# The first layer's output projection multiplies plain float32 operands once per product instead of rounded halves three times

## The chip, the cores and the metric

The kernel runs on one core of a Trainium2 chip, in one launch. The metric is device microseconds of that launch. The core's engines are TensorE (PE; its weight loads are shown apart as PEld), VectorE (DVE), ScalarE (ACT), GpSimd (POOL) and SyncE (SP), which here issues nearly all of the DMAs.

## What is computed

Two layers of a decoder trunk with three parallel attention branches. The sequence has 512 tokens, the model has 1024 channels, and everything is float32. The reference, cut to the lines that matter here:

```python
for layer in range(DEPTH):                       # DEPTH = 2
    h = rmsnorm(x, norm_g[layer])
    u = jnp.einsum('bsd,dc->bsc', h, w_in[layer])
    ... # three branches ya, yb, yc and their gates ga, gb, gc come out of u
    merged = (jax.nn.sigmoid(ga) * jnp.einsum('bsc,cd->bsd', ya, w_br_a[layer])
              + jax.nn.sigmoid(gb) * jnp.einsum('bsc,cd->bsd', yb, w_br_b[layer])
              + jax.nn.sigmoid(gc) * jnp.einsum('bsc,cd->bsd', yc, w_br_c[layer]))
    x = x + jnp.einsum('bsd,de->bse', merged, w_out[layer])
return rmsnorm(x, final_norm_g)
```

The change touches the product of `merged` with `w_out` for layer 0 alone: a matrix of 512 tokens by 1024 channels times one of 1024 by 1024.

## The kernel before, in words

Activations lie transposed, with 128 channels on the partitions and the 512 tokens along the free dimension. A matrix of 1024 channels is 8 tiles of 128x512.

**Three products for one.** Nearly every matmul works on numbers split in two: a high half, which is the value rounded to the type float32r, and a low half, which is what the rounding left, again as float32r. A product of two such numbers is three matmuls into the same accumulator, high by high, high by low and low by high (`mm3`, L125 to L128). An output tile of a projection is one accumulation over 8 channel tiles, 24 matmuls (`run_unit`).

**The weight stream.** All weights lie packed in one array, in blocks of 128x512 or so, in the order of their use. `dma_to` loads a block into a tile `raw`, of which there are 5 buffers (RAW). `split_to` makes the block's high half on ACT (a cast, L905) and its low half on DVE (a subtraction, L907), each into one of 6 buffers `wh` and `wl` (RING). This runs up to 6 blocks ahead of the matmuls. A `raw` buffer is free again when DVE has subtracted.

**The end of layer 0.** The last merge step for channel tile i (`m_item`, branch 2) leaves the finished sum `M[i]` in a float32 tile `mg`. ACT casts it to its high half (L605) and DVE subtracts for the low half (L606). These 16 half tiles lie in buffers named `qk` and `y`. Then comes the output projection, `o_item(e)` for e = 0 to 7. Each uses two weight blocks, named here oe-a (k = 0 to 3) and oe-b (k = 4 to 7). Its output is added to the residual, which was loaded as `xr` into a tile named `sz` (L626). The sum is stored to DRAM as `x1d` (L629), split for the next layer into `XH[e]` on ACT and `XL[e]` on DVE, and squared for the norm. Between these items stand the first steps of layer 1: `v_item(1, e-1)` is 12 matmuls with `XH[e-1]` and `XL[e-1]` and one more weight block (L229 to L231), named here v0 to v7. The order on PE is o0, o1, v0, o2, v1 and so on to o7, v6, v7. The norm's sums (L172) follow, then the step `va_item` with four blocks f0 to f3 (L256 to L258).

**What sets the order.** The kernel records its steps in a list and writes them out in that order, with the loads and splits of later blocks put between. A scheduler of the tile framework then orders each engine's queue and gives buffers out. Each engine works its queue strictly in order. SP issues the weight loads, the `xr` loads and the `x1d` stores from one queue.

**Plain float32 in the kernel before.** Three small products have both operands in plain float32: the norm's column sums (L172, 128x1, 16 matmuls in the program), the cumulative sum (L294, 128x16, 2 in the program) and its carries (L299, 128x12, 128x8 and 128x4, 6 in the program). L499, L323 and L213 are transposes.

The functions of the kernel before, where the diff touches them:

Of the kernel before, what the change touches and what calls it, by code (L numbers as in the profile page):

```python
# [13 lines left out]
P = 128  # L14
# [3 lines left out]
KT = 8  # L18
# [13 lines left out]
def _chunks():  # L32
    """Every weight block, in the order of the packed array: (key, floats per partition)."""
    out = []
    for l in range(L):
        for k in range(KT):
            out.append((("v", l, k), 512))
        for j in range(4):
            out.append((("f", l, j), 520))
        cols = []  # L40
        for n, w in (("qa", 2), ("ka", 2), ("za", 2), ("qb", 3), ("kb", 3), ("zb", 3),
                     ("qc", 3), ("kc", 1), ("zc", 3), ("ga", 8), ("gb", 8), ("gc", 8)):
            cols += [COL[n] + P * i for i in range(w)]
        for c in cols:
            for h in range(2):
                out.append((("u", l, c, h), 512))
        for br in range(3):
            for i in range(8):
                out.append((("p", l, br, i), P * NBR[br]))
        for e in range(8):  # L50
            for h in range(2):
                out.append((("o", l, e, h), 512))
    return out
# [11 lines left out]
def tile_trunk(ctx: ExitStack, tc: tile.TileContext, xT, wpk, gT, gfT, bfg, snk,  # L65
               mask_a, mask_b, mask_c, ident_d, upper_d, cos_d, sin_d, out):
    nc = tc.nc
# [13 lines left out]
    def mm_bank():  # L81
        return PS("mm", 3)
# [12 lines left out]

# [1 line left out]
    def const(src, shape, tag):  # L97
# [9 lines left out]

# [1 line left out]
    items = []  # L109
# [30 lines left out]

# [1 line left out]
    XH, XL = [None] * KT, [None] * KT  # L142
    st = {}
# [31 lines left out]
    def rms_post(tbs=range(4)):  # L175
        """1/sqrt(mean + eps) by token: a first guess from the bits, then Newton's steps."""
        c = slice(tbs[0], tbs[-1] + 1)
        v, t, vh = (T([P, 4], F32, n)[:, c] for n in ("rv", "rt", "rh"))
        seed = T([P, 4], I32, "r0")[:, c]
        st["r"] = T([P, 4], F32, "r")  # L180
        r = st["r"][:, c]
        nc.vector.tensor_scalar(v, st["ss"][:, c], 1.0 / D, EPS, op0=ALU.mult, op1=ALU.add)
        nc.vector.tensor_scalar(seed, v.bitcast(I32), -0.5, float(0x5F3759DF), op0=ALU.mult, op1=ALU.add)
        nc.vector.tensor_scalar(vh, v, -0.5, None, op0=ALU.mult)
        y = seed.bitcast(F32)
        for _ in range(3):
            nc.vector.tensor_tensor(t, y, y, op=ALU.mult)
            nc.vector.tensor_tensor(t, t, vh, op=ALU.mult)
            nc.vector.scalar_tensor_tensor(r, t, 1.5, y, op0=ALU.add, op1=ALU.mult)
            y = r  # L190

    def rms_root(tbs):
        """The same from the square root's table, with one of Newton's steps."""
        c = slice(tbs[0], tbs[-1] + 1)
        v, t, y = (T([P, 4], F32, n)[:, c] for n in ("rv", "rt", "rh"))
        st["r"] = T([P, 4], F32, "r")
        ss = st["ss"][:, c]
        nc.scalar.activation(y, ss, AF.Sqrt, scale=1.0 / D, bias=st["eps"])
        nc.vector.tensor_scalar(v, ss, -0.5 / D, -0.5 * EPS, op0=ALU.mult, op1=ALU.add)
        nc.vector.reciprocal(y, y)  # L200
        nc.vector.tensor_tensor(t, y, y, op=ALU.mult)
        nc.vector.tensor_tensor(t, t, v, op=ALU.mult)
        nc.vector.scalar_tensor_tensor(st["r"][:, c], t, 1.5, y, op0=ALU.add, op1=ALU.mult)
# [15 lines left out]

# [1 line left out]
    def v_item(l, k):  # L221
# [108 lines left out]

# [1 line left out]
    def qk_tile():  # L332
# [7 lines left out]
    def rope_1(ps):  # L340
        """The normalised values, their halves swapped, and the cosine's part."""
        x, sw, t = plain(ps), tmp(), tmp()
        for a, b in ((0, 32), (32, 0), (64, 96), (96, 64)):
            nc.sync.dma_start(sw[a:a + 32, :], x[b:b + 32, :])
        nc.gpsimd.tensor_tensor(t, x, st["cos"], op=ALU.mult)  # L345
        return t, sw
# [5 lines left out]
    def q_fill(t, h, aug):  # L352
        """Both heads' stacked q from t: high halves beside low halves."""
        for o in range(2):
            a, b = slice(HD * o, HD * o + HD), slice(HD - HD * o, 2 * HD - HD * o)
            q = st["QS", h + o] = qk_tile()
# [18 lines left out]

    # A projection is (chunks, pe, p1, p2, p3): the work of the other engines in three parts.
    def qk_item(l, kind, n, h):
        """Projection unit n of a kind of columns, whose heads are h and h+1."""
        rope = kind[1] != "a"
        fill = q_fill if kind[0] == "q" else k_fill  # L380
        d = {}
# [17 lines left out]

# [1 line left out]
    def z_item(l, kind, n, pair):  # L401
# [15 lines left out]

# [1 line left out]
    NSB = (2, 2, 3, 4)  # L419
# [148 lines left out]

# [1 line left out]
    def m_item(l, br, i):  # L570
# [18 lines left out]
        def p2():  # L589
# [7 lines left out]
            if br == 1:  # L597
                nc.gpsimd.tensor_tensor(m, m, gr, op=ALU.add)  # L598
                return
            nc.vector.tensor_tensor(m, m, gr, op=ALU.add)  # L600
            pair = []
            for w in range(2):
# [6 lines left out]

# [1 line left out]
    def load_res(e):  # L611
# [3 lines left out]
    def o_item(e):  # L615
        d = {}

        def pe(HL):
            if e == 0:
                load_res(0)  # L620
                load_res(1)
            d["ps"] = run_unit(HL, [st["MH", i] for i in range(8)], [st["ML", i] for i in range(8)])

# [10 lines left out]

    # The last layer's output projection goes by halves of the tokens, so that one half's norm and
    # store run beside the other half's products.
    HT = S // 2
# [80 lines left out]

# [1 line left out]
    xs = [T([P, S], F32, "mg", 8) for _ in range(KT)]  # L720
# [6 lines left out]
    def layer(l):  # L727
        if l == 0:
            for k in range(KT):
                v_item(0, k)  # L730
        # the later layers' V steps stand among the output projection's of the layer before
        pe, post, ch = va_item(l)
# [72 lines left out]
        a3, b_prev, v_prev = [], [], None  # L805
        # Scores run a head ahead of their transposes: h is the head whose scores follow.
        for h in range(17):
# [64 lines left out]

# [1 line left out]
    seq = [c for it in items for c in it[0] or ()]  # L874
# [12 lines left out]
    def places(key):  # L887
        """Where a block's two halves go; the last projection's all stay, where others have left."""
        n = 2 * key[2] + key[3] if key[:2] == ("o", L - 1) else 0
# [9 lines left out]
    def split_to(n):  # L899
        while ptr["split"] < min(n, len(seq)):  # L900
            i = ptr["split"]
            w = off[seq[i]][1]
            h, lo = places(seq[i])
            r = raw.pop(i)
            (nc.vector.tensor_copy if i == 0 else nc.scalar.copy)(h[:, :w], r[:, :w])  # L905
# [135 lines left out]
```

## Time and profile before

| What | Value |
|---|---|
| Median of 2 timed runs | 893.16 us (892.62 and 893.71) |
| Span of the profiled execution, first to last instruction | 891.6 us |
| What lies between that span and the median | 1.6 us |
| TensorE busy | 880.3 us, 99% of the span |
| VectorE busy | 607.0 us, 68% |
| ScalarE busy | 463.5 us, 52% |
| GpSimd busy | 127.4 us, 14% |
| Granted TensorE clock, mean | 0.996 of full speed |
| Share of PE in the chain that ended last | 97% |

The profiled execution has no time of its own on record besides its span; the two timed runs lie 1.0 and 2.1 us above it. Matmuls are pipelined: a row's duration reaches from the start of one matmul to its modelled end and overlaps with the next one's. What a matmul costs in a stream is therefore read from start to start.

### The profile page before, as it was taken

The page shows a single profiled execution, that of the slowest core. Times are in us where ns is not written, and L with a number is a line of the kernel's source. Part 1 is how long each engine was busy: PE and PEld are TensorE (multiplying, and loading weights), DVE is VectorE, ACT ScalarE, POOL GpSimd, SP SyncE. Part 2 cuts the span into 40 slices and gives each one's busy share as a digit, 9 for nine tenths or more (in the row PEclk, how much of TensorE's full clock was granted, in tenths as well). Part 3 has the DMA queues.
Part 4 walks back from the last instruction along what each step waited for, and adds up shares of the span by engine and source line. Part 5 has one row for each costly group of instructions (what it writes and reads, how often), then busy time and mean ns, then how long its engine had stood idle before and what let it go on. Part 6 is the DMA issues. An engine that isn't in the chain of part 4 may idle for free.

```text
span 891.6 us, 12997 instructions
## 1 busy us (share of the span) xinstructions
PE 880.3 (99%) x4432; PEld 740.6 (83%) x4432; DVE 607.0 (68%) x1280; ACT 463.5 (52%) x964; POOL 127.4 (14%) x98
## 2 busy tenths in 40 slices
PE   9999999999999999999999999999999999999996
PEld 7988888888888888888889888888888888888895
DVE  7658899898775646554445879999886655555433
ACT  7477566665554434334335766666554544333542
POOL 5000131211001110001120012212100111100531
PEclk9999999999999999999999999999999999999998
DMA  6532323323232323335542233233322332233423
GB/s 217 175 106 72 107 72 89 99 80 95 74 98 80 91 86 108 89 104 166 146 138 84 83 86 87 77 101 101 83 83 77 87 89 82 82 98 92 129 79 113
DMA packets 53875, 89.26 MB, mean 100 GB/s; under 512 B 7344, under 2 KB 15920, under 8 KB 53808
## 3 DMA queue, kind: packets, MB, share of 16 engines
q1 hardware_dynamic: 53664, 88.42, 34.6%
q8 instruction: 35, 0.57, 0.3%
q14 instruction: 32, 0.26, 0.1%
q10 hardware_dynamic: 144, 0.01, 0.0%
HBM read 78.96 MB, written 4.19 MB: 93 GB/s over the span
## 4 chain that ended last, share of the span: by engine, by line
PE 97%; DVE 1%; DMA 0%; issue 0%; ACT 0%; POOL 0%; DVEq 0%; ACTq 0%; POOLq 0%
PE mm L127 26%; PE mm L126 26%; PE mm L128 26%; PE pv L545 4%; PE att L499 3%; PE att L435 2%; PE att L434 2%; PE att L229 2%; PE att L230 2%; PE att L231 2%; PE mm L256 1%; PE mm L257 1%; PE mm L258 1%; DMA g<-in_gT_dram 0%; PE pv L172 0%
## 5 line engine op out<-in xcount | busy, mean ns | idle before, releaser
L126 PE MATMUL mm<-xh,wh 128*128 128x512 f32 x736 | 293.1, 398 | 0.0
L905 ACT CAST wh<-raw 128x512 fp32r<-128x512 f32 (+3 forms) x277 | 163.4, 593 | 246.9 <-PE mm L127 191.6
L128 PE MATMUL mm<-xh,wl 128*128 128x512 f32 x736 | 290.5, 395 | 0.0
L127 PE MATMUL mm<-xl,wh 128*128 128x512 f32 x736 | 290.0, 394 | 0.0
L907 DVE TENSOR_TENSOR wl<-raw,wh 128x512 fp32r<-128x512 f32 (+3 forms) x272 | 182.4, 672 | 66.7 <-ACT wh L905 65.9
L128 PEld LDWEIGHTS mm<-xh,wl 128*128 128x128 f32 x736 | 138.2, 188 | 32.6
L127 PEld LDWEIGHTS mm<-xl,wh 128*128 128x128 f32 x736 | 138.4, 188 | 30.4
L126 PEld LDWEIGHTS mm<-xh,wh 128*128 128x128 f32 x736 | 138.4, 188 | 30.1
L470 ACT ACTIVATE P<-P,ng 128x256 f32<-128x256 f32 (+3 forms) x128 | 67.0, 525 | 38.0 <-DVE ng L468 38.0
L586 DVE TENSOR_TENSOR tmp<-mm,rbc 128x512 f32<-128x512 f32 x48 | 33.1, 690 | 55.9 <-PE mm L128 55.9
L345 POOL TENSOR_TENSOR tmp<-tmp,cos 128x512 f32<-128x512 f32 x20 | 31.3, 1566 | 258.1 <-DVE tmp L337 241.6
L127 PE MATMUL mm<-y,wh 128*128 128x512 f32 (+1 forms) x156 | 60.1, 385 | 0.3 <-DVE y L606 0.3
L126 PE MATMUL mm<-y,wh 128*128 128x512 f32 (+1 forms) x156 | 60.3, 386 | 0.0
L128 PE MATMUL mm<-y,wl 128*128 128x512 f32 (+1 forms) x156 | 60.0, 385 | 0.0
L598 POOL TENSOR_TENSOR mg<-mg,tmp 128x512 f32<-128x512 f32 x16 | 25.8, 1611 | 235.9 <-DVE tmp L596 235.9
L525 DVE TENSOR_TENSOR PL<-att,PH 128x512 fp32r<-128x512 f32 (+2 forms) x84 | 46.5, 598 | 0.1
L587 ACT ACTIVATE tmp<-tmp 128x512 f32<-128x512 f32 x48 | 30.4, 634 | 23.7 <-DVE tmp L586 23.6
L596 DVE SCALAR_TENSOR_TENSOR tmp<-tmp,mm 128x512 f32<-128x512 f32 x32 | 22.0, 687 | 28.8 <-PE mm L128 27.6
L524 ACT CAST PH<-att 128x512 fp32r<-128x512 f32 (+2 forms) x84 | 39.5, 526 | 2.4 <-PE att L499 1.2
L488 DVE TENSOR_SCALAR P<-P,den 128x256 f32<-128x256 f32 (+3 forms) x128 | 38.4, 364 | 1.1
L435 PE MATMUL att<-qk,qk 128*128 128x256 f32 (+2 forms) x128 | 37.1, 309 | 0.1
L499 PEld LDWEIGHTS att<-ident,P 128*128 128x128 f32 x284 | 32.9, 141 | 4.1
(197 smaller groups left out, 1376.6 us busy)
## 6 DMA issues: line engine op xcount, KB each, us to landing
raw<-in_wpk_dram SPq DMA_DIRECT2D x232, 256.0 KB, 2.7
raw<-in_wpk_dram SPq DMA_DIRECT2D x32, 192.0 KB, 2.4
tmp<-tmp SPq DMA_DIRECT2D x80, 64.0 KB, 2.0
raw<-in_wpk_dram SPq DMA_DIRECT2D x8, 260.0 KB, 2.7
mg<-in_xT_dram SPq DMA_DIRECT2D x8, 256.0 KB, 5.6
raw<-in_wpk_dram SPq DMA_DIRECT2D x16, 128.0 KB, 2.1
sz<-in_xT_dram SPq DMA_DIRECT2D x8, 256.0 KB, 3.0
x1d<-tmp SPq DMA_DIRECT2D x8, 256.0 KB, 3.3
```

What stands on the lines that cost most here:

```text
L126: nc.tensor.matmul(ps, wh, xh, start=first, stop=False)
L127: nc.tensor.matmul(ps, wh, xl, start=False, stop=False)
L128: nc.tensor.matmul(ps, wl, xh, start=False, stop=last)
L435: nc.tensor.matmul(ps, q2[:, qs], k2[:, a:a + n], start=False, stop=True)
L470: nc.scalar.activation(pb, pb, AF.Exp, bias=ng[:, i:i + 1], scale=-1.0, accum_out=den[:, i:i + 1])
L488: nc.vector.tensor_scalar(blks[i], blks[i], den[:, i:i + 1], None, op0=ALU.mult)
L499: nc.tensor.transpose(ps[:, c * P:(c + 1) * P], pt[:, src * P:(src + 1) * P], st["ident"])
L524: nc.scalar.copy(hh, bk[:, :n])
L525: nc.vector.tensor_tensor(st["PL"][:, o:o + n], bk[:, :n], rd(hh), op=ALU.subtract)
L545: nc.tensor.matmul(ps[:, q:q + n], v[j], src[:, o:o + n], start=w == 0 and m == 0, stop=w == 1 and m == 3)
L905: (nc.vector.tensor_copy if i == 0 else nc.scalar.copy)(h[:, :w], r[:, :w])
L907: eng.tensor_tensor(lo[:, :w], r[:, :w], rd(h[:, :w]), op=ALU.subtract)
```

## The change

For layer 0 alone, the sum `M[i]` is no longer split, and the blocks of the output projection are no longer split. The projection's matmul takes the `raw` block and the tile `M[k]`, both plain float32, in one matmul per product. `split_to` hands a `raw` tile of this projection on as it is. Layer 1 keeps the three products. The diff, cut to its core (the rest of it removes comments and blank lines):

```diff
@@ m_item, p2
             nc.vector.tensor_tensor(m, m, gr, op=ALU.add)
+            if l == 0:
+                return
             pair = []
@@ o_item, pe
-            d["ps"] = run_unit(HL, [st["MH", i] for i in range(8)], [st["ML", i] for i in range(8)])
+            ps = d["ps"] = mm_bank()
+            for k in range(KT):
+                w = HL[k // 4][0]
+                nc.tensor.matmul(ps, w[:, (k % 4) * P:(k % 4 + 1) * P], st["M", k], start=k == 0, stop=k == KT - 1)
@@ split_to
             w = off[seq[i]][1]
+            r = raw.pop(i)
+            if seq[i][:2] == ("o", 0):
+                hl[i] = (r, r)
+                ptr["split"] += 1
+                continue
             h, lo = places(seq[i])
-            r = raw.pop(i)
```

In PE's queue, this is where the last merge step ends and o0 begins. In the names, `mm` is the accumulator, `y` and `qk` are halves of activations, `wh` and `wl` halves of weights. Before:

```order
L128 MATMUL mm_3991<-y_3544,wl_3948 128x512
L126 MATMUL mm_4032<-qk_3590,wh_4001 128x512
L127 MATMUL mm_4032<-qk_3591,wh_4001 128x512
L128 MATMUL mm_4032<-qk_3590,wl_4002 128x512
L126 MATMUL mm_4032<-qk_3650,wh_4001 128x512
L127 MATMUL mm_4032<-qk_3651,wh_4001 128x512
L128 MATMUL mm_4032<-qk_3650,wl_4002 128x512
```

And with the change, from the same place to the last two products of o1 and the first matmuls of v0:

```order
L128 MATMUL mm_3963<-y_3544,wl_3924 128x512
L627 MATMUL mm_3988<-mg_1717,raw_3871 128x512
L627 MATMUL mm_3988<-mg_1822,raw_3871 128x512
...
L627 MATMUL mm_4018<-mg_2727,raw_3929 128x512
L627 MATMUL mm_4018<-mg_2819,raw_3929 128x512
L229 MATMUL att_4047<-wh_3997,xh_877_4010 128x512
L230 MATMUL att_4047<-wl_3998,xh_877_4010 128x512
```

Each run of three rows has become one row, 64 rows in place of 192, and the steps keep their order on PE.

In SP's queue, this is a stretch of the weight loads in the first items of the projection, with what each load waits for in brackets. Before:

```order
L883 DMA raw_4069<-in_wpk_dram 128x512 [waits DMAHW0_49,DVE_49]
L883 DMA raw_4071<-in_wpk_dram 128x512 [waits DMAHW1_49,DVE_49]
L883 DMA raw_4084<-in_wpk_dram 128x512 [waits DMAHW2_49,DVE_49]
L883 DMA raw_4119<-in_wpk_dram 128x512 [waits DMAHW3_49,DVE_49]
L613 DMA sz_4075<-in_xT_dram 128x512 [waits DVE_49]
L629 DMA x1d<-tmp_4073 128x512
```

With the change (raw_3973 and raw_3975 are o2-a and o2-b, raw_3982 is v1, raw_4001 and raw_4003 are o3-a and o3-b, raw_4016 is v2):

```order
L888 DMA raw_3973<-in_wpk_dram 128x512 [waits DMAHW1_49,DVE_49]
L888 DMA raw_3975<-in_wpk_dram 128x512 [waits DMAHW5_49,PE_49]
L888 DMA raw_3982<-in_wpk_dram 128x512 [waits DMAHW6_49,PE_49]
L615 DMA sz_4007<-in_xT_dram 128x512 [waits DVE_49]
L634 DMA x1d<-tmp_4005 128x512
L888 DMA raw_4001<-in_wpk_dram 128x512 [waits DMAHW7_49,PE_49]
L888 DMA raw_4003<-in_wpk_dram 128x512 [waits DMAHW4_49,DMAHW0_49,DVE_49]
L888 DMA raw_4016<-in_wpk_dram 128x512 [waits PE_49]
L615 DMA sz_4035<-in_xT_dram 128x512 [waits DMAHW2_49,DVE_49]
```

Before, every weight load waits for DVE's subtraction of the block that held the buffer. Now two of three wait for PE, since the block of the projection stays in its buffer until its four matmuls are done: o2-b waits for the last matmul of o0-a, v1 for the last of o0-b, o3-a for the last of o1-a, v2 for the last of o1-b. The `xr` loads and `x1d` stores stand behind them.

## Rows read from the trace of the kernel before

**Rows 1.** The page's head and its first part, busy time by engine.
```profile
span 891.6 us, 12997 instructions
PE 880.3 (99%) x4432; PEld 740.6 (83%) x4432; DVE 607.0 (68%) x1280; ACT 463.5 (52%) x964; POOL 127.4 (14%) x98
```
**Rows 2.** Waits of PE in the whole run, all there are.
```profile
PE pv L917 <- DVE qk L914: 1.5, 1, 1.5
PE pv L213 <- DVE r L203: 1.3, 1, 1.3
PE pv L172 <- ACT tmp L676: 0.8, 1, 0.8
PE att L229 <- ACT ys L161: 0.7, 1, 0.7
PE mm L127 <- DVE y L606: 0.3, 1, 0.3
```
**Rows 3.** Busy time by engine from o0's first matmul to the norm's sums.
```profile
398.87:465.66 66.79, 66.79 (x289) 54.06 (x288) 29.84 (x44) 25.48 (x41) 9.93 (x10) 1.00 0.52 151
```
**Rows 4.** Instruction groups in that stretch: busy, mean, then idle before and its releasers.
```profile
L126 PE MATMUL mm<-qk,wh 128*128 128x512 f32 x48 | 18.9, 394 | 0.0
...
L907 DVE TENSOR_TENSOR wl<-raw,wh 128x512 fp32r<-128x512 f32 (+1 forms) x24 | 16.5, 689 | 20.3 <-ACT wh L905 20.3
L905 ACT CAST wh<-raw 128x512 fp32r<-128x512 f32 (+1 forms) x24 | 14.9, 622 | 36.0 <-PE mm L127 29.3 <-ACT tmp L164 6.0 <-ACT ys L161 0.6
```
**Rows 5.** Timeline of all engines around o0's start: start, duration, what.
```profile
398.87 0.40 PE L126 MATMUL mm<-qk,wh 128*128 128x512 f32 x1
...
400.34 0.68 DVE L600 TENSOR_TENSOR mg<-mg,tmp 128x512 f32<-128x512 f32 x1
...
401.71 0.69 DVE L606 TENSOR_TENSOR y<-mg,y 128x512 fp32r<-128x512 f32 x1 [0.69 <-ACT y L605]
```
**Rows 6.** PE groups by shape, whole run: float32r products, then plain float32 ones.
```profile
L545 PE MATMUL pv<-PL,vb 128*128 128x256 f32 x72 | 12.4, 281 | 0.0
L545 PE MATMUL pv<-PL,vb 128*128 128x512 f32 x12 | 4.8, 396 | 0.0
...
L299 PE MATMUL pv<-lf,ones 128*128 128x12 f32 x4 | 0.7, 259 | 0.0
L299 PE MATMUL pv<-lf,ones 128*128 128x8 f32 x4 | 0.7, 256 | 0.0
L299 PE MATMUL pv<-lf,ones 128*128 128x4 f32 x4 | 0.7, 253 | 0.0
L294 PE MATMUL pv<-lf,upper 128*128 128x16 f32 x4 | 0.6, 220 | 0.0
```
**Rows 7.** One line, L172: duration in ns (min, median, max).
```profile
L172 PE MATMUL pv<-ones,ys x24: 164/250/251, 30.2 to 882.7; 128*128 128x1 f32 x24
```
**Rows 8.** Timeline of PE around the first cumulative sum.
```profile
48.53 0.39 PE L128 MATMUL mm<-xh,wl 128*128 128x512 f32 x1
48.76 0.29 PE L294 MATMUL pv<-lf,upper 128*128 128x16 f32 x2
48.90 0.81 PE L299 MATMUL pv<-lf,ones 128*128 128x12 f32 x6
49.57 0.48 PE L126 MATMUL mm<-xh,wh 128*128 128x512 f32 x1
49.88 0.39 PE L127 MATMUL mm<-xl,wh 128*128 128x512 f32 x1
```
**Rows 9.** Timeline of the weight loads at the same place.
```profile
48.53 0.42 PEld L294 LDWEIGHTS pv<-lf,upper 128*128 128x128 f32 x2
48.87 0.75 PEld L299 LDWEIGHTS pv<-lf,ones 128*128 128x128 f32 x6
```
**Rows 10.** Weight-load groups by shape, whole run: float32r, then plain float32.
```profile
L126 PEld LDWEIGHTS mm<-xh,wh 128*128 128x128 f32 x736 | 138.4, 188 | 30.1
...
L172 PEld LDWEIGHTS pv<-ones,ys 128*128 128x128 f32 x24 | 3.3, 191 | 0.2
```
**Rows 11.** DMA issues, 395 to 480 us: count, size, median us to landing.
```profile
raw<-in_wpk_dram SPq DMA_DIRECT2D x27, 256.0 KB, 2.7
```

## The prediction

> **What bounds the kernel now.** I read the page's busy times first. PE is busy 880.3 of 891.6 us [rows 1]. The waits of PE say where the rest is: five waits, 4.6 us in all [rows 2], and what is left lies before the first and behind the last matmul. So the kernel is bound by the number and length of its matmuls. The reader should see that none of the five waits is in the projection itself: the one for L606 is of a later place, since in the stretch of the projection PE is busy for 66.79 of 66.79 us [rows 3].
>
> That stretch is the one to price. Its window begins with o0's first matmul and ends with the norm's sums, and holds the 192 matmuls of o0 to o7 and the 96 of v0 to v7 (the row's 289th is one that reaches in from ahead) [rows 3]. 66.79 us over 288 is **231.9 ns from start to start**. The mean of 394 ns that the group rows give [rows 4] is start to modelled end and overlaps with the next matmul, so it is not what one costs.
>
> **What is removed on PE.** 192 matmuls of 231.9 ns are 44.5 us. They lie fully on the path.
>
> **What is added on PE.** 64 matmuls of plain float32, 128x512. The trace of before has none of that width, and the nearest rows are the three small float32 products. Two things can be seen in them.
>
> First, one of them in the program is two in the trace. The program has 2 of L294, 6 of L299 and 16 of L172; the trace has 4 of L294 and three groups of 4 of L299, 12 in all [rows 6], and of L172 24 of the 12 that read `ys` [rows 7]. Each of the two has a weight load of its own: 2 loads for the one L294, 6 for the three L299 [rows 9]. So 64 matmuls in the program will be **128 in the trace**.
>
> Second, each of the two takes longer per column. For float32r, 256 columns have a duration of 281 ns and 512 have 396 [rows 6], which is 115/256 = 0.449 ns per column. (512 of those are 230 ns, which agrees with the 231.9 from start to start, so the growth of the duration with the columns is the rate, plus some 2 ns.) For float32 L299 has 253 ns at 4 columns, 256 at 8 and 259 at 12 [rows 6], and L172 250 at 1 [rows 7]: 9/11 = 0.82 ns per column, 1.8 times as much. The rows are rounded to a nanosecond, so that the slope may be 0.73 to 0.91; L294 (220 at 16) mixes a first and a second matmul and doesn't fit a line. A slope of that size means that each of the two streams its columns **at about half the rate**.
>
> So one matmul of 512 columns in the trace takes between 512 x 0.82 + 2 = 422 ns and, at exactly half the rate of float32r, 2 x 231.9 = 464 ns. I take the middle, 443 ns, as neither end has a better claim. A product is then 0.886 us (0.844 to 0.928), and 64 are **56.7 us** (54.0 to 59.4). A step from at most 16 columns to 512 is a long one, and this is the term on which the forecast rests. The Trainium skill speaks against the change here: "FP8 and Floating Point Precision", section "TensorE Precision Notes", says that true float32 takes four passes through the array, one for each pair of halves. No row here shows passes as such; by it the sum is an estimate of 64 x 4 x 231.9 ns = 59.4 us.
>
> **Switching between the types.** Behind the last L299 the first float32r matmul starts at 49.57 and the next one at 49.88, 0.31 us instead of 0.23 [rows 8]: 0.08 us more. The other way, from L128 to L294, it is 48.53 to 48.76, the usual 0.23 [rows 8]. The new order has seven changes from float32 to float32r (from o1 to v0, then from each of o2 to o7 to its v step), so 7 x 0.08 = **0.6 us**.
>
> **What goes from ACT and DVE.** 16 casts and 16 subtractions of weight blocks at 622 and 689 ns [rows 4], and eight of each for the sums M. This is some 24 x 0.62 = 15 us of ACT and 24 x 0.69 = 17 us of DVE. I cost it at nothing: PE, which is the bound, waits for neither in that stretch [rows 3], where they are busy for 25.48 and 29.84 of 66.79 us. The earlier M sums gain nothing either. Before, M[7] is summed from 400.34 to 401.02 and its low half is there at 402.40 [rows 5]; o0 asks for them as its eighth product, 7 x 0.695 = 4.9 us after 398.87. With the change it asks for M[7] at 398.87 + 7 x 0.886 = 405.1, 4 us after it is there.
>
> **What is moved on the queue of SP.** A block of the projection now holds its `raw` buffer until its matmuls are done, so that two of three weight loads wait for PE, with the `xr` loads and `x1d` stores queued behind them. Is a block late? A load lands 2.7 us after its issue [rows 11], and a v block then needs 0.62 us of ACT and 0.69 us of DVE [rows 4], 4.0 us in all. With products of 0.886 us an o item lasts 7.1 us and a v step 12 x 0.232 = 2.8 us. Block v1 waits for the end of o0, and is used after o1, v0 and o2, 17 us later. The `xr` tile of item 3 stands behind block v2, which waits for the end of o1; it is used at the end of o3, behind v0, o2, v1 and o3, 20 us later. The tightest is the row v6, v7, f1, which share one buffer: v6 waits for the end of o5, v7 for DVE's subtraction of v6, f1 for that of v7, at some 4.4 us each with the issue. f1's cast stands on ACT ahead of the split of o6's output, so that split comes 12 to 13 us after the end of o5; v6 uses it v4, o6, v5 and o7 after that end, 19.8 us. That leaves 6 us. So this costs 0, with 0 and 6 us as its ends, since a slip of the supply could not exceed the slack by more than one load and its split.
>
> **The sum.** 56.7 + 0.6 - 44.5 = **+12.8 us**, from 10.1 (54.0 + 0.6 - 44.5) to 15.5 (59.4 + 0.6 - 44.5). The profiled execution's span would become 904.4 us. With the 1.6 us between its span and the median, the time is 893.16 + 12.8 = **906.0 us**, 1.4% above before. A measurement of this kernel can tell about 2% from no change, that is 17.9 us, so that this counts as no change, on its slow side.
>
> **Rivals.** *The small products mislead, and each of the two matmuls streams at full rate.* Then 64 x 2 x 231.9 ns = 29.7 us, and the sum is 29.7 + 0.6 - 44.5 = -14.2: 879.0 us, or up to 882 where the supply of blocks, with an o item of only 3.7 us, is late by some load. For it: slopes over 11 columns are thin, and the ends of matmuls are modelled. Against it: four widths lie on one line. Chance 4%. That a wide float32 matmul is a single one in the trace would even give 64 x 231.9 ns = 14.8 us and 864 us; the counts of all three small products speak against it, 1%.
>
> *The weight loads come to light.* There are 128 of them, and a float32 load is 191 ns long [rows 10]. If such a load can't run beneath a float32 matmul, each costs up to 191 ns: 24.4 us on top of 12.8, 930.4 us, slower by 4.2%. It counts as slower from 5.1 us on, 40 ns per load. For it: no row shows a float32 load beneath a wide float32 matmul. Against it: L294's loads begin at 48.53, with L128's matmul and not after it, and the six of L299 take 0.75 us and not 6 x 0.19 = 1.14 [rows 9], so they overlap with each other and with float32 matmuls. Chance 7%. The Trainium skill has a rule on this side: "TensorE: Matmul & The Clock Gate", section "Weight-path perf modes", says that the fast weight load isn't used for FP32 input. Here the load of float32r is 188 ns and that of float32 191 [rows 10], so the trace shows no difference that would bear it out.
>
> *The supply of blocks is late.* An engine's queue that stands otherwise than I read it, above all ACT's casts of v7, f0 and f1 ahead of the split of o6's output, would put a wait of 3 to 6 us at v6 or v7, and some at each v step if it repeats: 909 to 918 us. It shows as a wait of PE at L229 for `xh`, or at L627 for a DMA. Chance 4%.
>
> **How the numbers follow.** The forecast has 84%, the rivals 5, 7 and 4%. The range goes from 901 to 912: the forecast's own 903.3 to 908.7, 1 to 2 us on either side for the spread of the runs and a slope at its limits, and the lower part of the late supply. What is left out above are the open weight loads and the rest of the late supply, below the full rate, together some 15%. Faster by over 2% (below 875.3) is only the single matmul, 1%. Slower by over 2% (above 911.0) are the weight loads, half of the late supply and an edge of the forecast, 11%. Within 2% remains 88%.
>
> **What would show it.** In the profile after: 128 matmuls of L627, at some 443 ns from start to start and in pairs; the stretch from o0 to the norm's sums 79.6 us long instead of 66.79; the first L229 behind each o item 0.31 us ahead of L230; no wait of PE in it; weight loads of L627 that begin during the matmul before them; casts of weight blocks in the stretch down from 24 to about 12, with no gain from it. The forecast is wrong if the start-to-start time of L627 is near 232 ns, or above 480, or if L229 waits for `xh` or a weight half.

## The result and the profile after

The changed kernel takes 903.5 us (median of 903.28 and 903.71), the kernel before 893.16 us. The ratio is 1.0115, with an interval of 1.0099 to 1.0131: 10.3 us slower, which is clear of the spread of the runs though below 2%. The forecast was 906.0 us, in a range of 901 to 912.

The page's head and busy times of the kernel after, which answer to [rows 1]:

```profile
span 901.5 us, 12787 instructions
PE 890.3 (99%) x4368; PEld 728.5 (81%) x4368; DVE 592.5 (66%) x1256; ACT 448.2 (50%) x940; POOL 126.6 (14%) x98
```

The span grew by 9.9 us and PE's busy time by 10.0, while ACT has 15.3 us less to do and DVE 14.5 us less. PE has 64 instructions fewer in the trace (192 went, 128 came). So the time is in PE's own work and not in a wait. The waits of PE say the same. They are the five of [rows 2], changed by 0.1 us at most:

```profile
PE pv L926 <- DVE qk L923: 1.5, 1, 1.5
PE pv L213 <- DVE r L203: 1.3, 1, 1.3
PE pv L172 <- ACT tmp L681: 0.9, 1, 0.9
PE att L229 <- ACT ys L161: 0.6, 1, 0.6
PE mm L127 <- DVE y L608: 0.3, 1, 0.3
```

Next the stretch from o0's first matmul to the norm's sums, by engine: length, then busy time and count of PE, PEld, DVE, ACT and POOL, the granted clock, DMA share and GB/s. It answers to [rows 3].

```profile
398.56:475.79 77.23, 77.23 (x226) 42.37 (x225) 22.34 (x31) 17.19 (x28) 9.21 (x9) 1.00 0.44 141
```

It was 66.79 us and is 77.23: **10.44 us longer, which is the whole difference.** (What lies outside the stretch is 0.5 us shorter than in the profile of before, which is less than it varies from run to run.) The clock is granted in full in both, 2.4 GHz. The 96 matmuls of v0 to v7 are the same as before, 96 x 231.9 ns = 22.26 us. What is left for the 128 of the projection is 54.97 us, 429.5 ns each.

The timelines of PE and of the weight loads at the start of the stretch (start, duration, what, and in brackets the idle time before it) show where that number can be read directly:

```profile
398.33 0.39 PE L128 MATMUL mm<-y,wl 128*128 128x512 f32 x1
398.56 13.89 PE L627 MATMUL mm<-mg,raw 128*128 128x512 f32 x32
411.90 0.80 PE L229 MATMUL att<-wh,xh 128*128 128x512 f32 x1
412.53 0.39 PE L230 MATMUL att<-wl,xh 128*128 128x512 f32 x1
```
```profile
398.34 0.42 PEld L627 LDWEIGHTS mm<-mg,raw 128*128 128x128 f32 x2
398.99 0.19 PEld L627 LDWEIGHTS mm<-mg,raw 128*128 128x128 f32 x1 [0.24 <-issue]
399.42 0.19 PEld L627 LDWEIGHTS mm<-mg,raw 128*128 128x128 f32 x1 [0.24 <-issue]
...
411.87 0.19 PEld L229 LDWEIGHTS att<-wh,xh 128*128 128x128 f32 x1 [0.24 <-issue]
```

o0 and o1, 16 products in the program, are 32 matmuls of L627 in the trace. The loads come once per matmul. From the third load (398.99) to that of L229, which is the 33rd (411.87), there are 30 steps in 12.88 us: 429.3 ns each. Each load is 0.19 us long and 0.24 us of idle time follow, so it lies wholly beneath the matmul ahead of it.

A wait can also stand with a weight load, where the list of PE's waits doesn't show it, as two of the experiments will show. So here are all waits of the weight loads in the stretch (in all, times, longest). "issue" is idle time in which the engine waited for nothing that the profile shows; none waits for a block, a half or another engine.

```profile
PEld mm L627 <- issue: 27.3, 114, 0.2
PEld att L229 <- issue: 1.7, 7, 0.2
PEld att L230 <- issue: 1.7, 7, 0.2
```

Read the start of that first L229 with care. It stands 0.63 us ahead of L230, and 0.23 us would be usual [rows 8]. But 32 matmuls of 429.4 ns end at 412.30, which is 0.23 us before L230. So the recorded start is 0.40 us ahead of the place where the matmul begins to cost anything, and no time is lost there.

The instruction groups in the stretch (busy time, mean, then idle time before), which answer to [rows 4]:

```profile
L627 PE MATMUL mm<-mg,raw 128*128 128x512 f32 x128 | 56.1, 592 | 0.0
...
L916 DVE TENSOR_TENSOR wl<-raw,wh 128x512 fp32r<-128x512 f32 (+1 forms) x12 | 9.0, 753 | 13.6 <-ACT wh L914 13.6
L914 ACT CAST wh<-raw 128x512 fp32r<-128x512 f32 (+1 forms) x12 | 7.4, 620 | 12.5 <-DMA raw<-in_wpk_dram 10.8 <-PE att L231 0.9 <-ACT tmp L164 0.8
```

The casts went from 24 to 12 and so did the subtractions. The mean of 592 ns is again start to modelled end.

### The profile page after: what moved, and what is told of

Same layout as the page of the kernel before. It is cut to its first block, busy times and chain, and to the rows that moved or that the text cites. A ratio compares the mean times of both kernels' runs of the same rounds, so it can differ in the third digit from the quotient of the medians.

```text
span 901.5 us, 12787 instructions
## 1 busy us (share of the span) xinstructions
PE 890.3 (99%) x4368; PEld 728.5 (81%) x4368; DVE 592.5 (66%) x1256; ACT 448.2 (50%) x940; POOL 126.6 (14%) x98
## 4 chain that ended last, share of the span: by engine, by line
PE 97%; DVE 1%; DMA 0%; issue 0%; ACT 0%; POOL 0%; DVEq 0%; ACTq 0%; POOLq 0%
PE mm L127 24%; PE mm L126 24%; PE mm L128 24%; PE mm L627 6%; PE pv L545 4%; PE att L499 3%; PE att L435 2%; PE att L434 2%; PE att L229 2%; PE att L230 2%; PE att L231 2%; PE mm L256 1%; PE mm L258 1%; PE mm L257 1%; DMA g<-in_gT_dram 0%
## 5 line engine op out<-in xcount | busy, mean ns | idle before, releaser
L126 PE MATMUL mm<-xh,wh 128*128 128x512 f32 x736 | 293.1, 398 | 0.0
L914 ACT CAST wh<-raw 128x512 fp32r<-128x512 f32 (+3 forms) x261 | 153.4, 591 | 232.2 <-PE mm L127 168.5
L916 DVE TENSOR_TENSOR wl<-raw,wh 128x512 fp32r<-128x512 f32 (+3 forms) x256 | 171.9, 674 | 70.8 <-ACT wh L914 70.0
L126 PEld LDWEIGHTS mm<-xh,wh 128*128 128x128 f32 x736 | 138.4, 188 | 30.2
L627 PE MATMUL mm<-mg,raw 128*128 128x512 f32 x128 | 56.1, 592 | 0.0
L127 PE MATMUL mm<-y,wh 128*128 128x512 f32 (+1 forms) x140 | 53.9, 385 | 0.3 <-DVE y L608 0.3
L126 PE MATMUL mm<-y,wh 128*128 128x512 f32 (+1 forms) x140 | 53.9, 385 | 0.0
L128 PE MATMUL mm<-y,wl 128*128 128x512 f32 (+1 forms) x140 | 53.6, 383 | 0.0
L627 PEld LDWEIGHTS mm<-mg,raw 128*128 128x128 f32 x128 | 24.3, 190 | 27.9 <-issue 27.3
```

The lines of the kernel that those rows point to most:

```text
L126: nc.tensor.matmul(ps, wh, xh, start=first, stop=False)
L127: nc.tensor.matmul(ps, wh, xl, start=False, stop=False)
L128: nc.tensor.matmul(ps, wl, xh, start=False, stop=last)
L627: nc.tensor.matmul(ps, w[:, (k % 4) * P:(k % 4 + 1) * P], st["M", k], start=k == 0, stop=k == KT - 1)
L916: eng.tensor_tensor(lo[:, :w], r[:, :w], rd(h[:, :w]), op=ALU.subtract)
```

## The experiments

The explanation that I set out to test: the change costs what its 128 matmuls stream, about 430 ns for 512 columns each, and neither a switch between types, nor the weight loads, nor ACT and DVE, nor the supply of blocks has a share. The rivals are that one of these has. What lies outside the stretch takes 823.5 to 825.2 us in the runs whose edit changes the projection alone. Most of that spread arises in the first 50 us: the first cumulative sum (L294) begins between 47.7 and 49.1 us. So stretch lengths are compared, and a difference of a microsecond between two spans is not a finding. A "stretch" is always o0's first matmul to the norm's sums, and 22.26 us of it are the v steps.

**One product instead of three (on the kernel before).** Only high by high is multiplied in layer 0's output projection; the other two products are left out. It asks whether a matmul taken away gives back its 231.9 ns.

```diff
-            d["ps"] = run_unit(HL, [st["MH", i] for i in range(8)], [st["ML", i] for i in range(8)])
+            ps = d["ps"] = mm_bank()
+            for k in range(KT):
+                w = HL[k // 4][0]
+                nc.tensor.matmul(ps, w[:, (k % 4) * P:(k % 4 + 1) * P], st["MH", k], start=k == 0, stop=k == KT - 1)
```

> The kernel before, with only the first of the three products (high half by high half) in layer 0's output projection; the other two products are left out, all splits are still made. Theory (PE is bound by the number of its matmuls there, 231.9 ns from start to start each): 128 matmuls less are 29.7 us, so a span of 891.6 - 29.7 = 861.9 us and no new wait of PE. Rival (the stream of weight blocks takes over as the bound once an item is short): an item then lasts 1.9 us and three blocks are needed every 4.6 us, PE waits for a weight half and the span is 864 us or more.

One run: 863.8 us, span 861.7, which is 29.9 us less. The stretch went from 66.79 to 38.18 us, 28.61 less. The 160 matmuls that are left in it need 37.10 us at 231.9 ns, so that 1.08 us are something else. The list of PE's waits has none in this stretch (0.4 us at L230, new in that list, lie in the first 30 us of the run, in layer 0's V steps). The weight loads' own waits in the stretch show it:

```profile
PEld att L229 <- ACT xh L152: 0.9, 2, 0.4
PEld att L231 <- DVE xl L155: 0.5, 1, 0.5
PEld mm L625 <- ACT y L605: 0.4, 1, 0.4
```

They wait for the halves of M[7] in o0, of o0's output at v0 and of o7's output at v7. By the starts of the matmuls PE loses 0.2, 0.3 and 0.6 us there. With these put aside, **the 128 matmuls gave back their 231.9 ns each.** Even with a projection this short no weight load waits for a block or for its halves; what comes late are the halves of activations.

**The casts and subtractions put back, unused (on the kernel after).** ACT and DVE do all the work of before, and PE still multiplies plain float32. It asks what their relief was worth.

```diff
             nc.vector.tensor_tensor(m, m, gr, op=ALU.add)
-            if l == 0:
-                return
...
             r = raw.pop(i)
-            if seq[i][:2] == ("o", 0):
-                hl[i] = (r, r)
-                ptr["split"] += 1
-                continue
...
-            hl[i] = (h, lo)
+            hl[i] = (r, r) if seq[i][:2] == ("o", 0) else (h, lo)
```

> The changed kernel, with the 16 casts and 16 subtractions of weight blocks and the 8 and 8 of the sums M put back, their results unused. Theory (the relief of ACT and DVE is worth nothing, as PE is the bound): the same time as the changed kernel, span 901.5 us within 0.5. Rival (the relief gave part of the four passes' cost back): slower by what it gave, 1 us or more.

903.8 us (median of 4), ratio 1.0123 with an interval of 1.0106 to 1.014; the change itself has 1.0115. The stretch of this kernel, in the columns of the window above:

```profile
399.16:476.34 77.18, 77.18 (x225) 42.35 (x224) 33.19 (x43) 24.28 (x40) 9.10 (x9) 1.00 0.48 141
```

DVE is busy for 10.9 us more than after and ACT for 7.1 more, and the stretch is 77.18 us against 77.23. **The relief is worth nothing.**

**256 and 128 columns at a time (on the kernel after).** Each product is cut into two or four matmuls over parts of the tokens. The columns in all stay the same, and the weight loads double or become four times as many.

```diff
             for k in range(KT):
                 w = HL[k // 4][0]
-                nc.tensor.matmul(ps, w[:, (k % 4) * P:(k % 4 + 1) * P], st["M", k], start=k == 0, stop=k == KT - 1)
+                for q in range(2):
+                    c = slice(q * S // 2, (q + 1) * S // 2)
+                    nc.tensor.matmul(ps[:, c], w[:, (k % 4) * P:(k % 4 + 1) * P], st["M", k][:, c],
+                                     start=k == 0 and q == 0, stop=k == KT - 1 and q == 1)
```

(The other has 4 in place of 2, and 3 in place of 1.)

> The changed kernel, each float32 matmul of 512 columns in two of 256. Theory (pure rate: 429.4 ns are 512 columns of 0.839 ns): 256 matmuls in the trace at 214.7 ns from start to start, span 901.5 us as before. Rival (a fixed part in each, with the slope of 0.82 ns per column that the small products showed: 429.4 = 512 x 0.82 + 9.6): 128 x 9.6 ns = 1.2 us more, 902.7 us. Second rival (the weight load of 190 ns is not hidden well): it has only 215 ns to hide in, several us more.

> The changed kernel, each float32 matmul of 512 columns in four of 128. Pure rate alone would give 107.4 ns each and 901.5 us. Theory with the weight loads as a floor (the small float32 products stand some 112 ns apart whatever their width): 512 matmuls x 112 ns = 57.3 us instead of 55.0, span 903.9 us. Rival with a fixed part of 9.6 ns: 384 x 9.6 ns = 3.7 us more, 905.2 us. Rival with loads that can't overlap (190 ns each): 97 us instead of 55, 944 us.

902.95 us (span 901.2) and 905.43 us (span 903.6), one run each. The groups and the stretch of the kernel with 256 columns:

```profile
L629 PE MATMUL mm<-mg,raw 128*128 128x256 f32 x256 | 56.4, 379 | 0.0
...
L629 PEld LDWEIGHTS mm<-mg,raw 128*128 128x128 f32 x256 | 48.6, 190 | 6.9
```
```profile
397.90:475.44 77.54, 77.54 (x354) 66.68 (x352) 22.44 (x31) 17.24 (x28) 9.21 (x9) 1.00 0.46 140
```

And of the one with 128:

```profile
L629 PE MATMUL mm<-mg,raw 128*128 128x128 f32 x512 | 58.3, 275 | 0.0
L629 PEld LDWEIGHTS mm<-mg,raw 128*128 128x128 f32 x512 | 58.3, 192 | 0.6
```
```profile
398.74:478.20 79.46, 79.46 (x610) 75.22 (x608) 22.36 (x31) 17.24 (x28) 9.23 (x9) 1.00 0.44 137
```

With twice the weight loads the stretch is 0.31 us longer, and neither PE nor a weight load has a wait in it (0.5 us at L230, new in the list of PE's waits, lie in the first 30 us of the run). So (77.54 - 22.26) / 256 = 215.9 ns for 256 columns, where half of 429.4 is 214.7 (o0 and o1 alone, 64 matmuls from 397.90 to 411.71, give 215.8). The 128 matmuls more cost 2.4 ns each, and between 256 and 512 columns the time grows by 0.834 ns per column: a small fixed part, and the rest is columns. With four times the loads it is (79.46 - 22.26) / 512 = 111.7 ns for 128 columns, where 128 x 0.834 + 2.4 is 109.2. Here the loads, 192 ns long each as recorded, overlap one another, with 0.6 us of idle time before all 512. The narrow products of before stood as far apart, whatever their columns: the six of L299 take from 48.90 to 49.57 [rows 8], 112 ns each. So at 128 columns something besides the columns begins to set the pace. That it is the weight loads fits but isn't shown. **At 512 and at 256 columns no load is in the open.**

**Plain float32 and three products in turn (on the kernel after).** Even channel tiles are multiplied as one float32 product, odd ones as three on halves, and all blocks of the projection are split again. That makes 32 changes from float32 to float32r within the projection, in place of 7.

```diff
-            if l == 0:
+            if l == 0 and i % 2 == 0:
                 return
...
-                w = HL[k // 4][0]
-                nc.tensor.matmul(ps, w[:, (k % 4) * P:(k % 4 + 1) * P], st["M", k], start=k == 0, stop=k == KT - 1)
+                c = slice((k % 4) * P, (k % 4 + 1) * P)
+                r, h, lo = HL[k // 4]
+                if k % 2 == 0:
+                    nc.tensor.matmul(ps, r[:, c], st["M", k], start=k == 0, stop=False)
+                else:
+                    mm3(ps, h[:, c], lo[:, c], st["MH", k], st["ML", k], False, k == KT - 1)
...
-            hl[i] = (h, lo)
+            hl[i] = (r, h, lo) if seq[i][:2] == ("o", 0) else (h, lo)
```

> Layer 0's projection with plain float32 for the even of the 8 products of an accumulation and the three products on halves for the odd ones; all weight blocks are split, and half of the sums M. Theory (429.4 ns per float32 matmul in the trace and no cost for changing the type): 32 products at 859 ns and 32 at 696 ns, 5.2 us more than before, a stretch of 72.0 us and a span of 896.8 us. Rival (0.08 us at each change from float32 to float32r, as the small products suggested): 32 changes, 2.6 us on top, 899.4 us.

One run: 897.66 us, span 895.9, and a stretch of 72.04 us (397.87 to 469.91). Its first matmuls on PE:

```profile
397.87 1.02 PE L629 MATMUL mm<-mg,raw 128*128 128x512 f32 x2
398.33 0.80 PE L126 MATMUL mm<-qk,wh 128*128 128x512 f32 x1
398.96 0.39 PE L127 MATMUL mm<-qk,wh 128*128 128x512 f32 x1
399.19 0.39 PE L128 MATMUL mm<-qk,wl 128*128 128x512 f32 x1
399.42 1.02 PE L629 MATMUL mm<-mg,raw 128*128 128x512 f32 x2
```

One float32 product and the three that follow take 1.55 us, from 397.87 to 399.42; 0.859 + 3 x 0.232 is 1.555. For the whole stretch, 32 x 0.859 us and the 192 float32r matmuls at 231.9 ns are 72.0 us. **A change of type costs nothing.** Here too the first matmul after the float32 ones (L126) is recorded 0.63 us ahead of the second.

**Four `raw` buffers instead of five (on the kernel after).** It asks how far the supply of blocks is from being late.

```diff
-RAW = 5
+RAW = 4
```

> The changed kernel with 4 instead of 5 buffers for weight blocks. Theory (blocks that stay in their buffers until the matmuls are done were 6 us or more ahead of their use): one buffer less takes up to one load with its split, 4 us, so no wait of PE for a block or for xh in the projection, span 901.5 us within 1. Rival (the supply was near its edge): waits of PE at L229 or L627 of 1 us or more per item, 908 us or more.

One run: 905.21 us, span 903.4. The stretch is 77.65 us, 0.42 longer than after. Again PE's own list has no wait in it (0.8 us at L230, new in that list, lie at 20.36 us, in layer 0's V steps). But two weight loads at v7 wait for the halves of o7's output, which they don't in the kernel after:

```profile
PEld att L231 <- DVE xl L155: 0.5, 1, 0.5
PEld att L229 <- ACT xh L152: 0.3, 1, 0.3
```

o7's matmuls end at 471.84, 0.23 us ahead of v6's second one, and DVE comes to its sum (L631) only 1.26 us later, behind the subtraction of a block whose cast had waited for its DMA; in the kernel after it comes 0.20 us behind that end.

```profile
471.82 0.63 ACT L914 CAST wh<-raw 128x520 fp32r<-128x520 f32 x1 [0.64 <-DMA raw<-in_wpk_dram]
...
472.48 0.70 DVE L916 TENSOR_TENSOR wl<-raw,wh 128x520 fp32r<-128x520 f32 x1 [0.56 <-ACT wh L914]
...
473.10 0.68 DVE L631 TENSOR_TENSOR tmp<-mm,sz 128x512 f32<-128x512 f32 x1
```

That blocks come later shows in the waits of ACT's casts between 395 and 490 us (in all, times, longest), first in the kernel after, then with four buffers:

```profile
ACT wh L914 <- DMA raw<-in_wpk_dram: 10.8, 9, 3.6
```
```profile
ACT wh L914 <- DMA raw<-in_wpk_dram: 46.7, 11, 6.9
```

So with one buffer less the blocks come late enough to hold up the split of an output, and it costs 0.4 us in this place. With five there is some to spare. The other 1.6 us by which o0 begins later than after (400.18) aren't the projection's: 1.5 of them are there at the first cumulative sum already (49.90 against 48.43), where runs with five buffers differ by nearly as much, so that they aren't shown to be the buffer's.

**bfloat16 halves in this projection (on the kernel before).** The halves of the weights and of M in layer 0's output projection are rounded to bfloat16 instead of float32r, so the product is coarser; the three matmuls stay. It was to tell whether 231.9 ns is what 512 columns cost, or whether a part of it belongs to the type.

```diff
-                pair.append(T([P, S], F32R, "qk", 12) if n < 12 else T([P, S], F32R, "y", 10))
+                t = T([P, S], F32R, "qk", 12) if n < 12 else T([P, S], F32R, "y", 10)
+                pair.append(t.bitcast(BF)[:, :S] if l == 0 else t)
...
+            bf = seq[i][:2] == ("o", 0)
+            if bf:
+                h, lo = h[:, :w].bitcast(BF)[:, :w], lo[:, :w].bitcast(BF)[:, :w]
...
```

> The kernel before, with the halves of layer 0's projection (weights and sums M) as bfloat16 instead of float32r; still three products, of which each is rounded more coarsely. It asks why one float32r matmul stands 231.9 ns from the next where a quarter of a plain float32 product is 214.7 ns. Theory (float32r has a cost of its own above the columns' rate): 192 matmuls at 215 to 216 ns, 3.1 us less, span 888.5 us. Rival (any single matmul with its own weight load costs 231.9 ns): span 891.6 us as before.

890.32 us (median of 6), ratio 0.9965 with an interval of 0.9952 to 0.9977; span 888.9. Its stretch, and a group of its weight loads:

```profile
399.38:463.21 63.83, 63.83 (x290) 36.50 (x289) 29.85 (x44) 25.37 (x41) 9.82 (x10) 1.00 0.52 157
```
```profile
L128 PEld LDWEIGHTS <-wh 128*128 128x128 bf16 x64 | 6.3, 98 | 6.7
```

(63.83 - 22.26) / 192 = 216.5 ns per matmul. So float32r takes some 15 to 16 ns more than bfloat16 for the same 512 columns. A weight load is 98 ns long and not 188 [rows 10], so the load was a suspect for those 16 ns.

**Narrow weights (on the kernel before).** Only high by high, and for six of the eight channel tiles with weights of 64 columns, three times over; the other two products and half of the output rows are left out. If the 16 ns belong to the weight load, a load of half the width would give a part of them back.

```diff
-            d["ps"] = run_unit(HL, [st["MH", i] for i in range(8)], [st["ML", i] for i in range(8)])
...
+                m = P if k in (0, KT - 1) else HD
+                for q in range(1 if m == P else 3):
+                    nc.tensor.matmul(ps[:m, :], w[:, c:c + m], st["MH", k], start=k == 0, stop=k == KT - 1)
```

> Layer 0's projection with the high halves alone in float32r; of the 8 products of an item the first and last have weights of 128 columns, the six between them weights of 64 columns, three times over, so 20 matmuls of 512 moving columns per item instead of 24. The other products and half of the output's rows are left out. It asks what makes a float32r matmul 16 ns longer than one of bfloat16. Theory A (the moving columns): 231.9 ns between all of them, 160 x 231.9 = 37.1 us instead of 44.5, span 884.2 us. Theory B (the weight load, 188 ns for 128 columns): the narrow ones stand 215 to 216 ns apart, 144 x 215.5 + 16 x 231.9 = 34.7 us, span 881.8 us.

One run: 885.4 us, span 883.6, and a stretch of 59.27 us: (59.27 - 22.26) / 160 = 231.3 ns, although the narrow load is shorter:

```profile
L628 PEld LDWEIGHTS mm<-qk,wh 128*64 128x64 f32 x120 | 16.1, 134 | 11.2
```

So the excess isn't the length of the weight load. That leaves the moving columns, or a fixed part of each matmul; the groups of the next run tell between them.

**bfloat16 halves in all projections (on the kernel before).** The same type for all halves of projections, V steps and merges in both layers; the attention stays float32r. All these products are coarser for it. If 16 ns per matmul is a price of the type, 2976 matmuls of 512 columns should give it back.

```diff
+    def H(tag, bufs=1):
+        return T([P, S], F32R, tag, bufs).bitcast(BF)[:, :S]
...
-        XH[k] = T([P, S], F32R, f"xh{k}")
-        XL[k] = T([P, S], F32R, f"xl{k}")
+        XH[k] = H(f"xh{k}")
+        XL[k] = H(f"xl{k}")
...
-            h, lo = places(seq[i])
+            h, lo = (t.bitcast(BF)[:, :w] for t in places(seq[i]))
...
```

> The kernel before, with the halves of all projections, V steps and merges in both layers as bfloat16 instead of float32r (attention keeps float32r); still three products each, rounded more coarsely. Theory (16.4 ns less for each of the 2976 matmuls of 512 columns and some 10 ns for 576 of 256 or 260): 48.8 + 5.8 = 54.6 us less, a span of 837 us. Rival (ACT and DVE, then busy for over 70% of the span, or the stream of weights come late more often): waits of PE that take a third or more of it back, 855 us or more.

844.2 us (median of 4), ratio 0.9458 with an interval of 0.9442 to 0.9474. It beats both kernels. The page's busy times and the first of PE's waits:

```profile
PE 827.3 (98%) x4432; PEld 460.9 (55%) x4432; DVE 602.1 (72%) x1280; ACT 459.7 (55%) x964; POOL 122.6 (15%) x98
```
```profile
PE att L439 <- POOL qk L378: 1.6, 2, 0.8
...
PE att L234 <- DVE wl L911: 1.1, 2, 0.9
```

PE's busy time fell by 53.0 us (880.3 to 827.3), and the span by 49.5 (891.6 to 842.1): PE is idle for 3.5 us more, as it now reaches places where POOL and DVE aren't done (of these, the 1.1 us at L234 lie in the first 30 us, where other runs had up to 0.8 as well). I had expected 5 us more of gain; 3.5 of them are these waits and 1.6 are matmul time that I counted too high.

Two groups of the run show where the excess of float32r lies:

```profile
L131 PE MATMUL mm<-qk,wh 128*128 128x512 bf16 x48 | 18.2, 379 | 0.0
...
L131 PE MATMUL mm<-qk,wh 128*128 128x256 bf16 x36 | 9.8, 272 | 0.0
```

From 256 to 512 columns the duration of a bfloat16 matmul grows by 107 ns, 0.418 per column; that of float32r grew by 115, 0.449 per column [rows 6]. Over 512 columns this is a difference of 16 ns, the whole excess. So by the recorded durations, whose ends are modelled, **float32r is slower per column**, and not by a fixed part. Why is open.

## Why the prediction held, step by step

- **What is removed.** 192 x 231.9 ns = 44.5 us was right; the first experiment got back 231.9 ns for each of 128, once its three waits are put aside.
- **Two in the trace for one in the program.** Right: 128 of L627, each with its own load.
- **How long each of them takes: the term that was mis-sized.** The forecast took 443 ns, the middle between 422 (the slope over 4 to 12 columns [rows 6]) and 464 (twice a float32r matmul). It is 429.4 ns, 0.839 ns per column. So the 64 products are 55.0 us and not 56.7. The low end, a slope and some 2 ns, had the right form: between 256 and 512 columns it is 0.834 ns per column and 2.4 ns. That its 0.82 came so near was in part luck, since the rounding of its rows allowed 0.73 to 0.91, which is 376 to 468 ns. The high end was wrong in kind, as the last experiments show: a float32r matmul carries 15 to 16 ns that a bfloat16 one doesn't (231.9 against 216.5), and the float32 one hasn't got them twice over. 429.4 is 1.98 times the bfloat16 matmul, and 1.85 times the float32r one.
- **Switching between types.** 0.6 us was forecast, and it is 0. With 429.3 ns from the loads, 64 x 0.8586 + 96 x 0.2319 = 77.21 us of the 77.23 that the stretch takes, and with 32 changes in turn nothing shows either. The sign that was named, a first L229 0.31 us ahead of L230, came out as 0.63 and means no time: a recorded start can stand too early. So it was with the 0.08 us in [rows 8]. Eight narrow float32 matmuls of 112 ns from 48.76 end at 49.65, which is the usual 0.23 us ahead of the second float32r one at 49.88.
- **The sum.** 55.0 - 44.5 = +10.5 us, against 10.44 in the stretch, 9.9 in the span and 10.3 in the timed medians. The forecast's +12.8 was 1.7 (the rate) and 0.6 (the switch) too high.
- **ACT and DVE: worth nothing.** Right, and shown by putting their work back. The relief was 15.3 and 14.5 us, where 15 and 17 were forecast, and the casts went down to 12 as forecast.
- **The supply of blocks: 0, with 6 us of slack at v6.** Right in the cost, and at v6. In the trace after, the split of o6's output runs on ACT and DVE behind the cast and the subtraction of later blocks:

```profile
462.11 0.63 ACT L914 CAST wh<-raw 128x520 fp32r<-128x520 f32 x1 [1.46 <-DMA raw<-in_wpk_dram]
462.64 0.72 ACT L152 ACTIVATE xh<-tmp,g 128x512 fp32r<-128x512 f32 x1
```
```profile
463.40 0.75 DVE L155 SCALAR_TENSOR_TENSOR xl<-tmp,g,xh 128x512 fp32r<-128x512 f32 x1
```
```profile
469.86 0.79 PE L229 MATMUL att<-wh,xh 128*128 128x512 f32 x1
470.49 0.39 PE L230 MATMUL att<-wl,xh 128*128 128x512 f32 x1
```

  The low half is there at 464.15, and v6 begins at 470.26, 0.23 us ahead of its L230: 6.1 us. The forecast's own figures, 19.8 us less 12 to 13, leave 6.8 to 7.8 and not the 6 that it wrote. But v6 isn't the tightest place, as the prediction had it. v7 uses the halves of o7's output, and only v6 stands between:

```profile
471.95 0.75 DVE L155 SCALAR_TENSOR_TENSOR xl<-tmp,g,xh 128x512 fp32r<-128x512 f32 x1 [0.79 <-ACT xh L152]
```
```profile
473.48 0.40 PE L231 MATMUL att<-wh,xl 128*128 128x512 f32 x1
```

  This low half is there at 472.70, 0.8 us ahead of its use, and with four buffers it was v7 that came late.
- **The rival of the full rate** would have needed 232 ns from start to start: refuted by 429. **The rival of the weight loads** needed 40 ns or more of each load in the open: none is, at 512 nor at 256 columns. **The rival of the late supply** has no wait to show in the stretch, of PE or of a weight load. Its mechanism is real: with four buffers it costs 0.4 us at v7, and shows only in the waits of the weight loads, not as the wait of PE that the prediction named.
- **The four passes.** The product of 0.859 us is 4 x 214.7 ns, and a bfloat16 matmul of the same width takes 216.5. The Trainium skill gives true float32 four passes through the array ("FP8 and Floating Point Precision", section "TensorE Precision Notes"). The trace agrees with that count in time, though it records two matmuls for a product and no passes. The estimate of 59.4 us that I drew from it was too high since it priced a pass at the float32r row; at 216.5 ns it would have been 55.4, against 55.0 measured.

## What to carry to other kernels

Where PE bounds the kernel, count what streams through it: one plain float32 product took 859 ns here, three float32r ones 696 and three bfloat16 ones 650, so that fewer instructions were more time, and some 15 us less on each of two engines with time to spare bought nothing. Don't price a matmul by a multiple of another type's row: the slope of small ones over their columns came nearer here, but a slope over 11 columns is only as good as its rounding, and one run at the width in question settles it. Read the cost of a matmul at a change of type from the stretch or from the weight loads, since its recorded start can lie early. And before you say that PE waits for nothing, look at the waits of the weight loads too, and at the time of each wait: the new waits at L230 lay in the first 30 us of the run, and the two losses in the projection, 1.08 and 0.42 us, stood under no wait of PE.

## What was unexpected of the hardware

- float32r isn't bfloat16's rate: 231.9 against 216.5 ns for 512 columns at the full clock, and weights of half the width don't change it (231.3). The excess grows with the columns (0.449 against 0.418 ns per column). Plain float32 has no such excess (429.4 ns, twice 214.7).
- The first float32r matmul behind float32 ones is recorded ahead of where it begins to take time, and the more so the wider these are: by 0.40 us behind 512 columns, 0.19 behind 256 (L229 at 411.52, L230 at 411.94), 0.08 behind 128 (412.95 and 413.26) and behind narrow ones [rows 8].
- A plain float32 weight load of 190 ns is hidden behind 256 columns (215.9 ns) and wider. At 128 columns matmuls stand 111.7 ns apart, as the narrow products do, with their loads overlapping one another.
